# One wide matmul in place of two narrow ones in the MLP and convolution projections of a decoder trunk

## The chip, the cores and the metric

The kernel runs on one core of one Trainium2 chip. The metric is device time in microseconds (us) of one execution; the medians below are over several executions. TensorE (PE in the tables) does the matmuls and has its weight loads listed apart (PEld); VectorE is DVE, ScalarE is ACT, GpSimd is POOL, and SP is the engine that issues most transfers. Matmul results go to PSUM, the accumulation memory, here in tiles of 512 fp32 columns (one bank) or 1024 (two banks); everything else lies in SBUF.

## The reference, cut to what matters

Four layers on 256 tokens of 1024 features. Each layer has a token mixer (stick-breaking attention, short convolution, gated linear attention, attention again) and an MLP with 4096 hidden features, each with an RMS norm before and after.

```python
def short_conv_mixer(xn, w_in, conv_w, w_out):
    bcu = xn @ w_in                                  # 1024 -> 3 x 1024
    b_gate, c_gate, u = jnp.split(bcu, 3, axis=-1)
    h = c_gate * u
    ...
    conv = sum(conv_w[i] * hp[:, i:i + s] for i in range(CONV_WIDTH))
    return (b_gate * conv) @ w_out

def squared_relu_mlp(xn, w_up, w_down):              # 1024 -> 4096 -> 1024
    return jnp.square(jax.nn.relu(xn @ w_up)) @ w_down
```

Everything is fp32. All weights, 213 MB, are read from HBM once.

## The kernel before, in words

**Precision.** TensorE is fed with a rounded fp32 format (fp32r). To keep fp32 accuracy each operand is split in two: hi is the value rounded to fp32r, lo is the rest. A product x·w is then three matmuls, hi(w)·hi(x), hi(w)·lo(x) and lo(w)·hi(x), added up in PSUM. Weights arrive as raw tiles of 128x1024 by transfers on SP (L197); `emit_upto` (L193) casts each on ScalarE to hi (L202) and subtracts on VectorE to get lo (L203), in two halves of 512 columns. The splits run six tiles ahead (LA), in rings of nine hi and nine lo tiles.

**Two ways to project.** `x_stat` (L307) keeps a 128x128 piece of x (or of the hidden features) stationary and streams 512 columns of weights; the results go to an acc tile of 1024 columns (two banks). `w_stat` (L358, steps from L346) keeps 128x128 pieces of the weights stationary and streams the 256 tokens of x; one unit makes 256 features for all 256 tokens in a wk tile (one bank): the two halves of 128 features lie side by side, and for each of 8 feature blocks k and each half j there are three matmuls of 256 columns, 48 in all. x lies transposed in two tiles, xth (its hi) and xtl (its lo).

**PSUM.** There are three acc tiles and two wk tiles, eight banks in all, and nothing else lies in PSUM. Tiles are handed out to whoever comes next once their last reader is done. The transposes (L262) that turn x or the hidden features also go through wk tiles, four of 128 columns to a tile.

**MLP (`ffn`, L395 on).** The hidden features come in eight groups of 512. Groups 0 and 1 are made by `up_x` with x stationary, then squared, and transposed. Groups 2 to 7 are made by `up_w`, two `w_stat` units each (k = 0, 1). After each unit ScalarE takes Relu out of the wk tile (L430), VectorE squares it (L431), ScalarE squares it again into hi (L434), VectorE subtracts for lo (L435). `down(g)` multiplies a group's hidden features by its part of the second weight and adds up in two acc tiles, one for each half of the tokens, from the first group to the last. `up_w(g)` is followed by `down(g - 2)`, so a group's features are wanted two groups later. In the last layer the second token half's sum takes one half of an acc tile and one half of the third.

**Convolution (`conv`, L594 on).** b is projected with x stationary and transposed (`turn`, L605). Then come four groups of 256 features: unit c in a wk tile, copied out by ScalarE (L618), and unit u in the other, multiplied by c on VectorE straight out of PSUM (L625). The three taps follow (L630, L632), the product with b (L636) and the split (L638), and after the fourth group the output projection. The attention and gated layers also use `w_stat` (for q and k).

**Order.** The code is written out in program order; a scheduler in the framework then orders each engine's instructions by priority and by its estimate of when operands and tiles are ready. Each engine runs its own row strictly in order. PE, DVE and ACT therefore meet at the tiles: PE waits for a wk or acc tile until it is copied out, and a copy waits for the unit's last matmul.

Of the kernel before, what the change touches and what calls it, by code (L numbers as in the profile page):

```python
# [9 lines left out]
F32 = mybir.dt.float32  # L10
F32R = mybir.dt.float32r
I32 = mybir.dt.int32
AF = mybir.ActivationFunctionType
ALU = mybir.AluOpType
PSUM = bass.MemoryType.PSUM

P = 128
D = 1024
UNIT = 1024
KT = D // P  # L20
SEQ = 256
# [40 lines left out]
def hybrid_kernel(ctx: ExitStack, tc: tile.TileContext, x, norm_gains, sb_w_qkv, sb_w_o,  # L62
# [5 lines left out]
    nc = tc.nc  # L68
# [6 lines left out]
    def pool(name, bufs, **kw):  # L75
        return ctx.enter_context(tc.tile_pool(name=name, bufs=bufs, **kw))

    cp = pool("const", 1)
# [10 lines left out]
    def nm(s):  # L89
        cnt[0] += 1  # L90
        return f"{s}{cnt[0]}"

    def T(pl, shape, dt, tag):
        return pl.tile(shape, dt, tag=tag, name=nm(tag))
# [4 lines left out]
    def acc_tile():  # L99
        return T(accp, [P, 1024], F32, "acc")  # L100

    def wk_tile():
        return T(wkp, [P, 512], F32, "wk")

    def slot(shape=(P, 1024), dt=F32):
        return T(slots, list(shape), dt, "s")

    def scratch():
        return slot()

    def mm(o, l, r, start, stop):
        nc.tensor.matmul(out=o, lhsT=l, rhs=r, start=start, stop=stop, skip_group_check=True)  # L112
# [39 lines left out]
    for kind, l in phases:  # L152
# [14 lines left out]
        elif kind == "sb":  # L167
            w = sb_w_qkv[l // 3]
# [5 lines left out]
        elif kind == "conv":  # L174
            w = conv_w_in[0]
# [5 lines left out]
        else:  # L181
            w = gla_w_in[0]
# [24 lines left out]
    def need(key, j=0):  # L207
        emit_upto(index[(key, j)] + 1 + LA)
        return ready[(key, j)]
# [11 lines left out]
    def split(hi, lo, src):  # L221
        nc.scalar.copy(out=hi, in_=src)  # L222
        nc.vector.tensor_tensor(out=lo, in0=src, in1=hi.bitcast(F32), op=ALU.subtract)
# [30 lines left out]
            if dst is not None:  # L254
                (nc.sync, nc.scalar)[n].dma_start(out=dst[:, cs], in_=h[t][:, cs])

    xth = T(cp, [P, KT, SEQ], F32R, "xth")
    xtl = T(cp, [P, KT, SEQ], F32R, "xtl")

    def transposes(src, dst, n):  # L260
        for j in range(n):
# [42 lines left out]
    def banks(acc):  # L304
        return [acc[:, 0:512], acc[:, 512:1024]]
# [52 lines left out]
    def w_stat(o, key):  # L358
        for _ in w_stat_steps(o, key):
            pass  # L360

    class Fill:


# [12 lines left out]
    def u_pair():  # L377
        return slot((P, 4, SEQ), F32R), slot((P, 4, SEQ), F32R)
# [16 lines left out]
    def ffn(l, finish, final=False):  # L395
        us = {}
        accs = [None, None]
        parts = {}

        def up_x():  # L400
            prs = [u_pair() for _ in range(XG)]
            for g in range(XG):
                us[g] = prs[g]
            for t in range(NT):
                acc = acc_tile()
                lh, ll = xs(t)
                for k in range(4):
                    un = [need((l, "up", g, k)) for g in range(XG)]
                    ws = [[(hi[:, a, :], lo[:, a, :]) for hi, lo in un] for a in range(2)]
                    for j, _ in enumerate(x_stat_steps(banks(acc), lh[2 * k:], ll[2 * k:], ws, k == 0, k == 3)):  # L410
                        if 2 * k + j + 1 == TURN[1]:
                            turn_pending()
                r = scratch()
                nc.scalar.activation(out=r, in_=acc, func=AF.Relu)
                s = scratch()
                nc.vector.tensor_tensor(out=s, in0=r, in1=r, op=ALU.mult)
                for g in range(XG):
                    w = wk_tile()
                    transposes(s[:, g * 512:], w, 4)
                    sl = (slice(None), slice(0, 4), slice(t * P, (t + 1) * P))  # L420
                    split(us[g][0][sl], us[g][1][sl], w.rearrange("p (a b) -> p a b", b=P))

        def up_w(g):
            us[g] = u_pair()
            for k in range(2):
                w = wk_tile()
                w_stat(w, (l, "up", g, k))
                rs = scratch()
                r, s = rs[:, 0:512], rs[:, 512:1024]
                nc.scalar.activation(out=r, in_=w, func=AF.Relu)  # L430
                nc.vector.tensor_tensor(out=s, in0=r, in1=r, op=ALU.mult)  # L431
                hi = us[g][0][:, 2 * k:2 * k + 2, :].rearrange("p a b -> p (a b)")
                lo = us[g][1][:, 2 * k:2 * k + 2, :].rearrange("p a b -> p (a b)")
                nc.scalar.activation(out=hi, in_=r, func=AF.Square)  # L434
                nc.vector.tensor_tensor(out=lo, in0=s, in1=hi.bitcast(F32), op=ALU.subtract)  # L435

        def down(g, ts_):
            for k in range(4):
                if 4 * (g - 6) + k == TURN[0]:
                    turn_pending()  # L440
                for t in ts_:
                    if accs[t] is None:
                        accs[t] = acc_tile()
                        parts[t] = banks(accs[t])
                        if final and t == NT - 1:
                            parts[t][1] = acc_tile()[:, 0:512]
                    sl = slice(t * P, (t + 1) * P)
                    x_stat(parts[t], [us[g][0][:, k, sl]], [us[g][1][:, k, sl]], [wide((l, "dn", g), k)],
                           g == 0 and k == 0, g == 7 and k == 3)

        up_x()
        for g in range(XG, 8):
            up_w(g)
            if g >= 2:
                down(g - 2, (0, 1))
        for t in range(NT):
            if final and t == NT - 1:
                for n in range(2):
                    for g in (6, 7):
                        for k in range(4):  # L460
                            sl = slice(t * P, (t + 1) * P)
                            x_stat(parts[t][n:], [us[g][0][:, k, sl]], [us[g][1][:, k, sl]],
                                   [wide((l, "dn", g), k)[n:n + 1]], False, g == 7 and k == 3)
            else:
                down(6, (t,))
                down(7, (t,))
            finish(parts[t] if final and t == NT - 1 else [accs[t]], t)
# [126 lines left out]
    def conv(l, finish):  # L594
        cw = T(cp, [P, 3, KT], F32, "cw")
        nc.gpsimd.dma_start(out=cw, in_=conv_w[0].rearrange("i (k p) -> p i k", p=P))
        bt = [slot((P, 4, SEQ)) for _ in range(2)]
        bs = []
        for t in range(NT):
            acc = x_proj(t, (l, "b"))  # L600
            b = scratch()
            nc.scalar.copy(out=b, in_=acc)
            bs.append(b)

        def turn(t):  # L605
            for half in range(2):
                w = wk_tile()
                transposes(bs[t][:, half * 512:], w, 4)
                nc.vector.tensor_copy(out=bt[half][:, :, t * P:(t + 1) * P], in_=w.rearrange("p (a b) -> p a b", b=P))  # L609

        turn(0)
        us = [u_pair(), u_pair()]
        for g in range(4):
            w = wk_tile()
            w_stat(w, (l, "c", g))
            cs = scratch()
            c, y = cs[:, 0:512], cs[:, 512:1024]
            nc.scalar.copy(out=c, in_=w)  # L618
            if g == 0:
                turn(1)  # L620
            w = wk_tile()
            w_stat(w, (l, "u", g))
            hp = slot((P, 2, SEQ + 2))
            nc.gpsimd.memset(hp[:, :, 0:2], 0.0)
            nc.vector.tensor_tensor(out=hp[:, :, 2:SEQ + 2], in0=w.rearrange("p (a b) -> p a b", b=SEQ),  # L625
                                    in1=c.rearrange("p (a b) -> p a b", b=SEQ), op=ALU.mult)
            for j in range(2):
                f = 2 * g + j
                yj = y[:, j * SEQ:(j + 1) * SEQ]
                nc.scalar.activation(out=yj, in_=hp[:, j, 0:SEQ], func=AF.Copy, scale=cw[:, 0, f:f + 1])  # L630
                for i in (1, 2):
                    nc.vector.scalar_tensor_tensor(out=yj, in0=hp[:, j, i:i + SEQ], scalar=cw[:, i, f:f + 1],  # L632
                                                   in1=yj, op0=ALU.mult, op1=ALU.add)
            btv = bt[g // 2][:, 2 * (g % 2):2 * (g % 2) + 2, :].rearrange("p a b -> p (a b)")
            yb = scratch()[:, 0:512]
            nc.vector.tensor_tensor(out=yb, in0=y, in1=btv, op=ALU.mult)  # L636
            sl = (slice(None), slice(2 * (g % 2), 2 * (g % 2) + 2), slice(None))
            split(us[g // 2][0][sl].rearrange("p a b -> p (a b)"), us[g // 2][1][sl].rearrange("p a b -> p (a b)"), yb)  # L638
        out_proj(l, us, finish)
# [207 lines left out]
    k, l = phases[0]  # L847
# [64 lines left out]
```

## Time and profile before

| | |
|---|---|
| median of three runs | 1217.8 us (1217.74 to 1217.99) |
| profiled execution | 1217.98 us |
| its span, first to last instruction | 1216.1 us |
| PE busy | 1190.9 us, 98% of the span, 7260 matmuls |
| weight loads (PEld) busy | 1051.6 us, 86% |
| VectorE, ScalarE, GpSimd busy | 63%, 55%, 4% |
| mean granted TensorE clock | 0.998 of 2.4 GHz |
| HBM read | 213.01 MB, 176 GB/s over the span |

The profile is of one execution. A matmul's row gives its start and how long it lasted to the last result; successive matmuls overlap, so a stream's speed is read from the distance between starts, or from the length of an unbroken run of matmuls divided by their number. The chain that ended last is followed back from the last instruction, at each step to what released it. A row names output and inputs without buffer numbers, `wk<-xth,hi` being a matmul into a wk tile that streams xth against a stationary hi.

### The profile page before, as it was taken

Reading aid. Unit: us, or ns where it says so; the run is one execution under the profiler, and the core shown is the slowest. Engines: PE = TensorE matmul, PEld = TensorE weight load, DVE = VectorE, ACT = ScalarE, POOL = GpSimd, SP = SyncE. Lnnn points to the kernel's source line nnn. Section 1 sums busy time; section 2 is a strip of 40 time slices with the busy share of each in tenths; the row PEclk is TensorE's granted clock in tenths of the full one; section 3 lists DMA queues with packets and bytes.
Section 4 is the critical chain, followed back from the end, with each engine's and each line's share of the span. In section 5 each row is a group of like instructions: output and inputs, shape, how many; then the busy total and the mean of one; then the engine's idle time right before and its main releaser. Section 6 shows DMA issues by size and latency. Waiting matters only on the chain.

```text
span 1216.1 us, 18811 instructions
## 1 busy us (share of the span) xinstructions
PE 1190.9 (98%) x7260; PEld 1051.6 (86%) x7260; DVE 770.4 (63%) x1203; ACT 670.2 (55%) x1192; POOL 52.4 (4%) x90
## 2 busy tenths in 40 slices
PE   5999999999999999999999999999999999999997
PEld 4998889988889888998789888989988988899986
DVE  6675776555677766555656677655558666765552
ACT  5687565554555465554464645645545876564451
POOL 2000100000100100000200110000000000000000
PEclk9999999999999999999999999999999999999999
DMA  7843457566466556666564346665647452666640
GB/s 237 273 123 120 139 191 217 185 190 222 140 208 191 173 187 215 189 191 208 162 221 133 94 135 223 192 196 185 208 140 236 128 157 95 198 211 194 188 153 35
DMA packets 123083, 215.28 MB, mean 177 GB/s; under 512 B 7729, under 2 KB 85681, under 8 KB 122994
## 3 DMA queue, kind: packets, MB, share of 16 engines
q1 hardware_dynamic: 122434, 213.28, 55.8%
q8 instruction: 57, 0.93, 0.3%
q0 software_dynamic: 128, 0.21, 0.1%
q10 hardware_dynamic: 432, 0.59, 0.1%
q14 instruction: 32, 0.26, 0.1%
HBM read 213.01 MB, written 1.05 MB: 176 GB/s over the span
## 4 chain that ended last, share of the span: by engine, by line
PE 93%; issue 3%; ACT 1%; DVE 1%; DMA 1%; POOL 1%; SPq 0%; DVEq 0%; POOLq 0%; ACTq 0%
PE acc L112 54%; PE wk L112 37%; PE wk L262 2%; DMA raw<-in_sb_w_qkv_dram 1%; DMA raw<-in_gla_w_in_dram 0%; ACT hi L202 0%; POOL sm L232 0%; ACT s L559 0%; ACT s L237 0%; POOL s L784 0%; DVE lo L203 0%; DVE s L279 0%; POOL sm L229 0%; DVE h L253 0%; ACT s L797 0%
## 5 line engine op out<-in xcount | busy, mean ns | idle before, releaser
L203 DVE TENSOR_TENSOR lo<-raw,hi 128x512 fp32r<-128x512 f32 x768 | 500.9, 688 | 265.0 <-ACT hi L202 261.1
L202 ACT CAST hi<-raw 128x512 fp32r<-128x512 f32 x768 | 442.7, 618 | 355.2 <-PE wk L112 169.1
L112 PE MATMUL acc<-hi,s 128*128 128x512 f32 x1280 | 355.1, 392 | 0.0
L112 PE MATMUL wk<-xth,hi 128*128 128x256 f32 x1216 | 342.1, 281 | 0.4 <-DVE s L609 0.4
L112 PE MATMUL wk<-xtl,hi 128*128 128x256 f32 x1216 | 341.9, 281 | 0.0
L112 PE MATMUL wk<-xth,lo 128*128 128x256 f32 x1216 | 341.3, 281 | 0.0
L112 PEld LDWEIGHTS acc<-hi,s 128*128 128x128 f32 x1280 | 237.4, 188 | 48.9 <-ACT s L222 1.3
L112 PEld LDWEIGHTS wk<-xth,hi 128*128 128x128 f32 x1216 | 229.3, 189 | 2.5 <-issue 0.7
L112 PEld LDWEIGHTS wk<-xtl,hi 128*128 128x128 f32 x1216 | 229.1, 188 | 1.3 <-issue 0.2
L112 PEld LDWEIGHTS wk<-xth,lo 128*128 128x128 f32 x1216 | 229.5, 189 | 0.2 <-issue 0.2
L112 PE MATMUL acc<-lo,s 128*128 128x512 f32 x640 | 199.7, 390 | 0.0
L112 PEld LDWEIGHTS acc<-lo,s 128*128 128x128 f32 x640 | 120.0, 188 | 25.3
L112 PE MATMUL acc<-hi,xth 128*128 128x512 f32 x288 | 94.0, 404 | 1.2 <-ACT xth L222 1.2
L112 PE MATMUL acc<-hi,xtl 128*128 128x512 f32 x288 | 93.0, 401 | 0.0
L112 PE MATMUL acc<-lo,xth 128*128 128x512 f32 x288 | 92.3, 400 | 0.0
L112 PEld LDWEIGHTS acc<-hi,xtl 128*128 128x128 f32 x288 | 54.7, 190 | 12.9
L112 PEld LDWEIGHTS acc<-lo,xth 128*128 128x128 f32 x288 | 54.6, 191 | 12.9
L112 PEld LDWEIGHTS acc<-hi,xth 128*128 128x128 f32 x288 | 53.9, 191 | 13.4 <-ACT xth L222 1.6
L250 DVE TENSOR_TENSOR s<-acc,s 128x1024 f32<-128x1024 f32 (+1 forms) x17 | 19.7, 1161 | 65.3 <-ACT s L237 65.0
L229 POOL TENSOR_SCALAR sm<-sm 128x1 f32<-128x1 f32 (+1 forms) x32 | 15.2, 476 | 1053.8 <-ACT s L237 1049.1
L112 PE MATMUL acc<-s,s 128*128 128x256 f32 (+3 forms) x316 | 51.5, 336 | 2.3 <-ACT s L559 1.8
L237 ACT ACTIVATE s<-acc 128x1024 f32<-128x1024 f32 (+1 forms) x17 | 16.6, 974 | 63.3 <-PE acc L112 63.3
(102 smaller groups left out, 762.9 us busy)
## 6 DMA issues: line engine op xcount, KB each, us to landing
raw<-in_ffn_w_up_dram SPq DMA_DIRECT2D x128, 512.0 KB, 3.8
raw<-in_ffn_w_down_dram SPq DMA_DIRECT2D x128, 512.0 KB, 3.6
raw<-in_sb_w_qkv_dram SPq DMA_DIRECT2D x48, 512.0 KB, 4.9
raw<-in_conv_w_in_dram SPq DMA_DIRECT2D x24, 512.0 KB, 4.4
raw<-in_gla_w_in_dram SPq DMA_DIRECT2D x24, 512.0 KB, 4.4
s<-in_norm_gains_dram SPq DMA_DIRECT2D x16, 512.0 KB, 5.1
raw<-in_sb_w_o_dram SPq DMA_DIRECT2D x16, 512.0 KB, 3.7
raw<-in_conv_w_out_dram SPq DMA_DIRECT2D x8, 512.0 KB, 3.6
```

Of the source, the lines that this page charges most:

```text
L112: nc.tensor.matmul(out=o, lhsT=l, rhs=r, start=start, stop=stop, skip_group_check=True)
L202: nc.scalar.copy(out=hi[:, cs], in_=raw[:, cs])
L203: nc.vector.tensor_tensor(out=lo[:, cs], in0=raw[:, cs], in1=hi[:, cs].bitcast(F32), op=ALU.subtract)
L229: nc.gpsimd.tensor_scalar(out=v, in0=ss, scalar1=EPS, scalar2=None, op0=ALU.add)
L237: nc.scalar.activation(out=scratch()[:, 0:src.shape[1]], in_=src, func=AF.Square, scale=1.0 / 32.0, accum_out=ss)
L250: nc.vector.tensor_tensor(out=ag[:, cs], in0=a, in1=g[:, cs], op=ALU.mult)
L262: nc.tensor.transpose(out=dst[:, j * P:(j + 1) * P], in_=src[:, j * P:(j + 1) * P], identity=ident)
```

## The change

x's hi and lo now lie side by side in one tile xt, 512 columns for each feature block, and xth and xtl are views of it. A new helper `w_wide` makes the same unit as `w_stat` with two matmuls in place of three for each k and j: hi(w) against both parts of x in one matmul of 512 columns, then lo(w) against hi(x), 256 columns, added onto the second half. The unit now takes two banks, one for each half j of its features, and its result is the sum of the first and the second half of a bank. `w_sum` makes that sum: ScalarE copies the second half out of PSUM and VectorE adds the first half to it. The unit's PSUM is an acc tile (k = 0 of each MLP group; c and u of the convolution) or both wk tiles (k = 1). The MLP's units then take max(y, 0)·y in one VectorE operation and split it with a cast and a subtraction. In the last layer the k = 1 units stay as they were and one wk tile holds the half sum that lay in the third acc tile. q and k of the attention and gated layers are not changed.

```diff
-    xth = T(cp, [P, KT, SEQ], F32R, "xth")
-    xtl = T(cp, [P, KT, SEQ], F32R, "xtl")
+    xt = T(cp, [P, KT, 2, SEQ], F32R, "xt")
+    xth, xtl = xt[:, :, 0, :], xt[:, :, 1, :]
...
+    def w_wide(key, two):
+        if two:
+            parts = [wk_tile().rearrange("p (j b) -> p j b", j=1) for _ in range(2)]
+            o = [p[:, 0, :] for p in parts]
+        else:
+            parts = [acc_tile().rearrange("p (j b) -> p j b", j=2)]
+            o = [parts[0][:, j, :] for j in range(2)]
+        for k in range(KT):
+            hi, lo = need(key, k // 4)
+            for j in range(2):
+                cs = slice(j * P, (j + 1) * P)
+                mm(o[j], hi[:, k % 4, cs], xt[:, k, :, :].rearrange("p c s -> p (c s)"), k == 0, False)
+                mm(o[j][:, SEQ:2 * SEQ], lo[:, k % 4, cs], xth[:, k, :], False, k == KT - 1)
+        return parts
+
+    def w_sum(parts, out, small_out):
+        n = 2 // len(parts)
+        for j, part in enumerate(parts):
+            js = slice(j * n, (j + 1) * n)
+            nc.scalar.copy(out=small_out[:, js, :], in_=part[:, :, SEQ:2 * SEQ])
+            nc.vector.tensor_tensor(out=out[:, js, :], in0=part[:, :, 0:SEQ], in1=small_out[:, js, :], op=ALU.add)
...
             for k in range(2):
-                w = wk_tile()
-                w_stat(w, (l, "up", g, k))
...
+                if final and k == 1:
...
+                    continue
+                parts = w_wide((l, "up", g, k), k == 1)
+                ys = scratch().rearrange("p (c j b) -> p c j b", c=2, j=2)
+                y, s = ys[:, 0, :, :], ys[:, 1, :, :]
+                w_sum(parts, y, s)
+                nc.vector.scalar_tensor_tensor(out=s, in0=y, scalar=0.0, in1=y, op0=ALU.max, op1=ALU.mult)
+                split(us[g][0][:, 2 * k:2 * k + 2, :], us[g][1][:, 2 * k:2 * k + 2, :], s)
...
-                            parts[t][1] = acc_tile()[:, 0:512]
+                            parts[t][1] = wk_tile()
...
-            w = wk_tile()
-            w_stat(w, (l, "c", g))
...
-            nc.scalar.copy(out=c, in_=w)
+            halves = lambda ap: ap.rearrange("p (a b) -> p a b", b=SEQ)
+            w_sum(w_wide((l, "c", g), False), halves(c), halves(y))
             if g == 0:
                 turn(1)
-            w = wk_tile()
-            w_stat(w, (l, "u", g))
+            ub = scratch()
+            u = halves(ub[:, 0:512])
+            w_sum(w_wide((l, "u", g), False), u, halves(ub[:, 512:1024]))
...
-            nc.vector.tensor_tensor(out=hp[:, :, 2:SEQ + 2], in0=w.rearrange("p (a b) -> p a b", b=SEQ),
-                                    in1=c.rearrange("p (a b) -> p a b", b=SEQ), op=ALU.mult)
+            nc.vector.tensor_tensor(out=hp[:, :, 2:SEQ + 2], in0=u, in1=halves(c), op=ALU.mult)
```

Three places show what this does to the order. In these rows a number behind a name tells tiles apart and has no other meaning.

PE at the start of the first MLP, before: acc_1789 and acc_1804 are the two sums of down(0), the two L262 rows transpose group 0 and group 1 for the second half of the tokens, and wk_1649 is the first up unit.

```order
L112 MATMUL acc_1789<-hi_1530,s_1431 128x512 x2
L112 MATMUL acc_1789<-lo_1531,s_1431 128x512 x2
L112 MATMUL acc_1789<-hi_1530,s_1432 128x512 x2
L262 MATMUL wk_1633<-cf_84,s_1631 128x128 x4
L262 MATMUL wk_1640<-cf_84,s_1631 128x128 x4
L112 MATMUL acc_1789<-hi_1652,s_1431 128x512
L112 MATMUL acc_1804<-hi_1522,s_1431 128x512 x2
L112 MATMUL acc_1804<-lo_1523,s_1431 128x512 x2
L112 MATMUL acc_1789<-hi_1652,s_1431 128x512
L112 MATMUL acc_1789<-lo_1653,s_1431 128x512
L112 MATMUL wk_1649<-xth_93,hi_1466 128x256
```

PE at the same place now, in two pieces: around the transposes (acc_1648 is the first up unit, k = 0), and where the second unit, k = 1, begins in wk_1703 and wk_1704.

```order
L112 MATMUL acc_1648<-xt_93,lo_1466 128x256
L112 MATMUL acc_1648<-xt_93,hi_1465 128x512
L263 MATMUL wk_1632<-cf_84,s_1630 128x128 x4
L263 MATMUL wk_1639<-cf_84,s_1630 128x128 x4
L112 MATMUL acc_1648<-xt_93,lo_1466 128x256
L112 MATMUL acc_1648<-xt_93,hi_1473 128x512
```

```order
L112 MATMUL acc_1648<-xt_93,hi_1473 128x512
L112 MATMUL acc_1648<-xt_93,lo_1474 128x256
L112 MATMUL wk_1703<-xt_93,hi_1493 128x512
L112 MATMUL wk_1703<-xt_93,lo_1494 128x256
L112 MATMUL wk_1704<-xt_93,hi_1493 128x512
```

The matmuls of down(0) that stood around the transposes have moved behind the up units; fifteen matmuls of the first up unit stand ahead of the transposes and seventeen behind them, and the k = 1 unit takes over the two wk tiles that the transposes leave.

PE in the convolution at the second turn of b, before: wk_3401 is unit c of group 0, wk_3480 its unit u.

```order
L112 MATMUL wk_3401<-xth_93,lo_3251 128x256
L262 MATMUL wk_3468<-cf_84,s_3383 128x128 x4
L262 MATMUL wk_3474<-cf_84,s_3383 128x128 x4
L112 MATMUL wk_3480<-xth_93,hi_3264 128x256
L112 MATMUL wk_3480<-xtl_94,hi_3264 128x256
```

The same place now, with the units c and u in acc_3239 and acc_3303.

```order
L112 MATMUL acc_3239<-xt_93,hi_3087 128x512
L112 MATMUL acc_3239<-xt_93,lo_3088 128x256
L263 MATMUL wk_3290<-cf_84,s_3220 128x128 x4
L263 MATMUL wk_3296<-cf_84,s_3220 128x128 x4
L112 MATMUL acc_3303<-xt_93,hi_3101 128x512
L112 MATMUL acc_3303<-xt_93,lo_3102 128x256
```

The order is the same; the units no longer share the two wk tiles with the transposes.

VectorE behind the first two up units, before: L431 squares, L435 subtracts, L203 are weight splits.

```order
L431 TENSOR_TENSOR s_1714<-s_1714 128x512
L203 TENSOR_TENSOR lo_1793<-raw_1790,hi_1792 128x512
L435 TENSOR_TENSOR s_1648<-s_1714,s_1647 128x512
L203 TENSOR_TENSOR lo_1814<-raw_1811,hi_1813 128x512 x2
L203 TENSOR_TENSOR lo_1834<-raw_1831,hi_1833 128x512
L431 TENSOR_TENSOR s_1784<-s_1784 128x512
L203 TENSOR_TENSOR lo_1834<-raw_1831,hi_1833 128x512
L435 TENSOR_TENSOR s_1648<-s_1784,s_1647 128x512
```

VectorE there now: L386 adds the halves, L469 squares, L223 subtracts.

```order
L386 TENSOR_TENSOR s_1697<-acc_1648,s_1697 128x512
L203 TENSOR_TENSOR lo_1765<-raw_1762,hi_1764 128x512
L469 SCALAR_TENSOR_TENSOR s_1697<-s_1697 128x512
L203 TENSOR_TENSOR lo_1786<-raw_1783,hi_1785 128x512
L223 TENSOR_TENSOR s_1647<-s_1697,s_1646 128x512
L203 TENSOR_TENSOR lo_1786<-raw_1783,hi_1785 128x512
L386 TENSOR_TENSOR s_1753<-wk_1703,s_1753 128x256
L203 TENSOR_TENSOR lo_1806<-raw_1803,hi_1805 128x512
L386 TENSOR_TENSOR s_1753<-wk_1704,s_1753 128x256
L203 TENSOR_TENSOR lo_1806<-raw_1803,hi_1805 128x512
L469 SCALAR_TENSOR_TENSOR s_1753<-s_1753 128x512
```

One addition per unit is new, in two pieces for a k = 1 unit, each with a copy on ScalarE ahead of it, and the weight splits stand between the steps as before.

## Rows read from the trace of the kernel before

**Rows 1.** The page's busy times: us (share of the span), instructions.

```profile
PE 1190.9 (98%) x7260; PEld 1051.6 (86%) x7260; DVE 770.4 (63%) x1203; ACT 670.2 (55%) x1192; POOL 52.4 (4%) x90
```

**Rows 2.** The page's chain that ended last: shares by engine, then by line.

```profile
PE 93%; issue 3%; ACT 1%; DVE 1%; DMA 1%; POOL 1%; SPq 0%; DVEq 0%; POOLq 0%; ACTq 0%
PE acc L112 54%; PE wk L112 37%; PE wk L262 2%; DMA raw<-in_sb_w_qkv_dram 1%; DMA raw<-in_gla_w_in_dram 0%; ACT hi L202 0%; POOL sm L232 0%; ACT s L559 0%; ACT s L237 0%; POOL s L784 0%; DVE lo L203 0%; DVE s L279 0%; POOL sm L229 0%; DVE h L253 0%; ACT s L797 0%
```

**Rows 3.** The page's groups: first of three narrow kinds; busy, mean ns | idle before.

```profile
L112 PE MATMUL wk<-xth,hi 128*128 128x256 f32 x1216 | 342.1, 281 | 0.4 <-DVE s L609 0.4
```

**Rows 4.** The chain by time: start us, length us, what ran.

```profile
186.33 11.39 PE wk L112 x96
197.73 10.91 PE acc L112 x48
...
331.28 11.23 PE acc L112 x48
```

**Rows 5.** Timeline of PE, attention of layer 0: start, length in us, instruction.

```profile
119.67 0.53 PE L112 MATMUL acc<-s,cr 128*128 128x256 f32 x2
120.03 0.28 PE L112 MATMUL acc<-s,onesr 128*128 128x256 f32 x1
120.15 0.52 PE L112 MATMUL acc<-s,cr 128*128 128x256 f32 x2
120.51 0.28 PE L112 MATMUL acc<-s,onesr 128*128 128x256 f32 x1
```

**Rows 6.** Timeline of PE, an earlier head pair of the same layer.

```profile
103.72 0.39 PE L112 MATMUL acc<-s,cr 128*128 128x512 f32 x1
103.95 0.28 PE L112 MATMUL wk<-xth,hi 128*128 128x256 f32 x1
104.06 0.28 PE L112 MATMUL acc<-s,onesr 128*128 128x256 f32 x1
...
105.23 0.51 PE L112 MATMUL acc<-s,cr 128*128 128x256 f32 x2
105.58 0.28 PE L112 MATMUL acc<-s,onesr 128*128 128x256 f32 x1
```

**Rows 7.** Timeline of PE at the start of the first MLP's up units.

```profile
165.38 1.06 PE L262 MATMUL wk<-cf,s 128*128 128x128 f32 x8
166.20 1.21 PE L112 MATMUL acc<-hi,s 128*128 128x512 f32 x3
167.24 0.63 PE L112 MATMUL acc<-lo,s 128*128 128x512 f32 x2
```

**Rows 8.** Timeline of VectorE at the same place.

```profile
166.95 1.28 DVE L223 TENSOR_TENSOR s<-wk,s 128x512 fp32r<-128x512 f32 x2
```

**Rows 9.** Timeline of PE, start of the convolution; in brackets, idle before and its releaser.

```profile
345.18 0.38 PE L112 MATMUL wk<-xth,hi 128*128 128x256 f32 x1 [0.41 <-DVE s L609]
...
352.16 0.66 PE L262 MATMUL wk<-cf,s 128*128 128x128 f32 x4 [0.64 <-ACT s L618]
```

**Rows 10.** Stretches: length; PE, PEld, DVE, ACT, POOL busy; clock, DMA share, GB/s.

```profile
352.80:392.70 39.90, 39.90 (x338) 39.90 (x337) 28.72 (x50) 20.64 (x39) 0.00 (x0) 1.00 0.58 176
...
197.70:220.00 22.30, 22.30 (x146) 20.41 (x145) 12.77 (x20) 11.17 (x21) 0.00 (x0) 1.00 0.62 189
```

**Rows 11.** Groups by form, whole span: operations that price the evictions; busy, mean ns.

```profile
L625 DVE TENSOR_TENSOR s<-wk,s 128x512 f32<-128x512 f32 x4 | 2.8, 692 | 3.9 <-PE wk L112 3.9
L277 DVE SCALAR_TENSOR_TENSOR s<-h,sm,s 128x512 f32<-128x512 f32 x2 | 1.4, 750 | 0.7 <-DMA s<-in_norm_gains_dram 0.7
...
L618 ACT COPY s<-wk 128x512 f32<-128x512 f32 x4 | 2.3, 581 | 0.0
```

**Rows 12.** The convolution's end: VectorE's last subtraction, and the chain's output projection.

```profile
397.62 0.69 DVE L223 TENSOR_TENSOR s<-s,s 128x512 fp32r<-128x512 f32 x1 [0.69 <-ACT s L222]
...
392.69 19.07 PE acc L112 x84
```

More of the change, by code (lines that the diff above doesn't have):

```diff
@@ L425, in up_w @@
             for k in range(2):
-                w = wk_tile()
-                w_stat(w, (l, "up", g, k))
[L428 to L435, printed above, removed]
+                if final and k == 1:
+                    w = wk_tile()
+                    w_stat(w, (l, "up", g, k))
+                    rs = scratch()
+                    r, s = rs[:, 0:512], rs[:, 512:1024]
+                    nc.scalar.activation(out=r, in_=w, func=AF.Relu)
+                    nc.vector.tensor_tensor(out=s, in0=r, in1=r, op=ALU.mult)
+                    hi = us[g][0][:, 2 * k:2 * k + 2, :].rearrange("p a b -> p (a b)")
+                    lo = us[g][1][:, 2 * k:2 * k + 2, :].rearrange("p a b -> p (a b)")
+                    nc.scalar.activation(out=hi, in_=r, func=AF.Square)
+                    nc.vector.tensor_tensor(out=lo, in0=s, in1=hi.bitcast(F32), op=ALU.subtract)
+                    continue
[5 more added lines that the diff above has]
+                split(us[g][0][:, 2 * k:2 * k + 2, :], us[g][1][:, 2 * k:2 * k + 2, :], s)
         def down(g, ts_):
```

## The prediction, made before the changed kernel ran

> **What bounds the kernel now.** I read the page's busy times first: PE is busy for 98% of the span, VectorE for 63%, ScalarE for 55% [rows 1]. A busy PE may still stand on pipelined matmuls, so next comes the chain that ended last: 93% of it is PE, 54% matmuls into acc tiles and 37% into wk tiles, all issued at L112 [rows 2]. From about 20 us to 1200 us, PE therefore runs one matmul behind the other and sets the time. What counts is then not how long one matmul lasts (its 0.28 or 0.39 us overlap the next) but the distance between starts, which the chain by time gives: 96 narrow matmuls (256 columns) of two up units in 11.39 us, **118.7 ns each**; 48 of 512 columns in a down step in 10.91 us, **227.3 ns**; 48 of 512 columns that have x as the stationary side in 11.23 us, **234.0 ns** [rows 4]. At the full clock, 2.4 GHz (the mean granted clock is 0.998), 256 columns take 106.7 ns and 512 take 213.3, so there is a fixed part per matmul of 12.0, 14.0 and 20.7 ns. That fixed part is all that the change can save: the columns stay.
>
> **The change, part by part.**
> *Matmuls.* Each of the three kinds of narrow matmul (hi by xth, hi by xtl, lo by xth) stands 1216 times in the trace [rows 3]. The new helper serves 42 up units (six groups, two units, four layers, less the six k = 1 units of the last layer) and 8 convolution units, with 16 triples in each: 50 x 16 = 800 triples become pairs of one 512 column and one 256 column matmul. 800 matmuls and 800 weight loads go. A triple now costs 3 x 118.7 = 356.0 ns.
>
> A pair of 512 and 256 columns in regular alternation does not stand in the trace. Bounds: the settled streams give 227.3 + 118.7 = 346.0 ns [rows 4]; with the dearer of the two 512 prices, 352.7. Nearest in kind are the attention's suffix sums, where single 512s stand among 256s: 256 then 512 takes 0.36 us twice (119.67 to 120.03, 120.15 to 120.51) [rows 5], and 512 then 256 takes 0.34 us (103.72 to 104.06), 256 then 512 0.35 us (105.23 to 105.58) [rows 6]: 352.5 ns on average. In alternation the pattern is regular, as in the settled streams, but lengths change at each step, as in the mixed rows. I take **350 ns**, between 346 and 352.5 and a little nearer to the mixed ones. The saving is 6.0 ns x 800 = **4.8 us**, between 8.0 us at 346 and a loss of 0.8 to 3.2 us at 357 to 360, which the mixed rows do not exclude.
>
> On this fixed part the Trainium skill (TensorE: Matmul & The Clock Gate, section Back-to-back issue gap) says otherwise: N/2.4 plus about 2.5 ns. By that an estimate for the triple is 327.5 ns and for the pair 325.0, a gain of 2.0 us in all. The trace differs, with a fixed part of 12 to 21 ns [rows 4], so the page's price is not used.
>
> *Waits at the start of an MLP.* Today the two transposes of step t = 1 (165.38) are followed by matmuls of down that need what is copied out of these transposes: the next five starts, from 166.20, should be 227 ns apart, but the first three take until 167.24, 1.04 us for 0.68 [rows 7]. In the new order the first up unit, now in an acc tile, stands on both sides of the transposes and needs nothing of them: 0.36 us x 4 layers = **1.4 us** less. What is late next: the k = 1 unit takes both wk tiles, which the transposes hold until VectorE's second subtraction ends at 166.95 + 1.28 = 168.23 [rows 8], 1.8 us after the transposes end (166.44). Before it come 17 matmuls of the first unit, 8 x 350 + 119 = 2.9 us. That covers it with 1.1 us to spare.
>
> *Waits at the start of the convolution.* PE waits 0.41 us for the copy out of a wk tile before unit c0, and 0.64 us for ScalarE's copy out of c0's wk tile before the second pair of transposes [rows 9]. With c0 in an acc tile, neither buffer is wanted there: **1.05 us** less. The weights of c0 were split before those copies, so nothing else is known to be late. If some other wait comes, these two terms (2.45 us in all) are what it can take back.
>
> *Evictions.* An up unit had on ScalarE a Relu and a Square, on VectorE a product and a subtraction; it gets a copy and a cast on ScalarE, and on VectorE an addition more. The prices: 0.58 us for a copy of 128x512 out of PSUM, 0.69 for a two-input VectorE operation out of PSUM, up to 0.75 for the three-operand form [rows 11]. So VectorE gets about 0.75 us per up unit, 1.5 us per group (a little more for k = 1, which is copied and added in two pieces); it is busy for 12.77 of 22.30 us there [rows 10] and comes to 14.5. In the convolution each group of c and u gets 1.4 us on VectorE, at 28.72 of 39.90 us now for 3.5 groups [rows 10], so about 33.5 of 39 us. Both are hidden under PE. The results of an up unit are wanted two groups later, behind 11 us of down. The tightest place is the end of the convolution: the last subtraction ends at 397.62 + 0.69 = 398.31, and PE wants it after 36 of the 84 matmuls that start at 392.69, 8.2 us on, at 400.9 [rows 12]. The new copy and addition, with a weight split between, add about 1.5 us to 2.6 us of slack. I cost all evictions at nothing; without that cover this place would cost what exceeds the slack, under 1 us.
>
> *Layout, queues.* xt holds hi and lo of x side by side; its writers and readers keep their shapes. The order of the weight transfers on SP stays the same, and these run at 0.62 of the DMA engines in the up stretch [rows 10]: nothing.
>
> *Sum* against the profiled execution, 1217.98 us (span 1216.1): 1217.98 - 4.8 - 1.4 - 1.05 = 1210.73. The median of the runs, 1217.8, is 0.18 us below that execution, so the forecast is **1210.6 us**; the rivals are reckoned from the median too.
>
> **The rivals.**
> *A: the alternation settles as well as the long streams,* 346 ns for a pair, as the down steps do after their first few matmuls. For it: a regular pattern. Against it: no mixed stretch shows it steadily. 8.0 + 2.45 us less: 1207.3.
> *B: the 512 column matmul costs what it costs with x on the stationary side,* 234.0, a pair 352.7 ns [rows 4]. For it: the mean of the mixed rows is the same; against it: here x moves and the weights stand, as in the settled narrow stream. 2.6 + 2.45 us less: 1212.7.
> *B2: only 2 to 3 ns go with the matmul, the rest of the fixed part with the columns;* the pair then costs about 353.5 ns, 2.0 + 2.45 us less: 1213.4. Against it: 14.0 ns at 512 columns and 12.0 at 256 in the settled streams [rows 4]. The section of the Trainium skill named above would give this time.
> *C: the change does not do what it says:* the fixed part goes with the columns alone. 512 columns then cost 2 x 118.7 = 237.4 ns, not far from the 234.0 of the third stream [rows 4], and a pair 356 to 358; only the waits go. For it also: 0.36 us for such pairs [rows 5]. At 357 ns 0.8 us more, less 2.45: 1216.1 (1215.4 to 1217.0), within 0.2% of before but for its lower edge.
> *D, slower: alternation is dearer than the triple.* The place is every pair, the price what exceeds 356.0 ns. Rows 5 show 0.36 us for a pair, which by the rounding of the start times may be anything from 350 to 370. At 364: 800 x 8 = 6.4 us more, less 2.45: 1221.7. It decides over 0.2% from (2.4 + 2.45)/0.8 = 6.1 ns on, at 362 ns for a pair. Against it: rows 6, at 0.34 and 0.35.
>
> **How the numbers follow.** A measurement of this kernel can tell about 0.2% (2.4 us) from no change. Forecast 0.40, A 0.22, B 0.14, B2 0.06, C 0.12, D 0.06. Faster by more than 0.2% are the forecast, A, B and B2: 0.82. Within it C: 0.12. Slower D: 0.06. The range takes in A with a pair of 344 ns (9.6 us, if the 512 keeps the 12.0 ns of the narrow stream), which gives 1205.7, B and B2, and reaches halfway into C: **1205.5 to 1216.5**.
>
> **What would show it.** In the changed trace the up unit (32 matmuls) should take about 5.6 us in place of 5.7, so that a group's two units last 11.2 us where they lasted 11.39; this alone decides between the forecast (11.20), A (11.07), B and B2 (11.29, 11.31), C (11.4) and D (11.65). The count of PE's matmuls should fall by about 800. At an MLP's start the three matmuls behind the transposes should no longer stretch, and the k = 1 unit should begin without a wait; if PE waits there for VectorE, the cover of 2.9 us was too short. At the convolution both waits should be gone, and the output projection should run through its 36th matmul without a gap. VectorE's share in the up stretch should rise to about 0.65 of the time, with PE still without gaps. The prediction would be wrong if PE showed new waits on wk or acc tiles in every group, or if a pair came out beyond 357 ns.

## The result and the profile after

The changed kernel takes **1205.7 us** (median of 4 runs, 1205.0 to 1207.1) beside 1217.8 for the kernel before: ratio 0.990, 95% interval 0.989 to 0.991. That is 12 us faster; the forecast was 7.2 us faster, and the median lies only 0.2 us inside the lower edge of its range, 1205.5. The profiled execution took 1205.45 us (span 1203.6) at a granted clock of 0.997.

The page's busy times and the shares of its chain, to be read beside [rows 1] and [rows 2]:

```profile
PE 1180.6 (98%) x6460; PEld 1010.5 (84%) x6460; DVE 803.0 (67%) x1271; ACT 673.9 (56%) x1214; POOL 51.8 (4%) x90
...
PE 93%; DMA 2%; issue 1%; ACT 1%; DVE 1%; POOL 1%; SPq 0%; DVEq 0%; POOLq 0%; ACTq 0%
```

PE has 800 matmuls and 800 weight loads fewer, as the change says, and is as full as before: 98% of a shorter span, 93% of the chain. VectorE rose from 63 to 67%; no new wait of PE for it appeared (the list of waits below).

The chain by time, the view of [rows 4]: start, length, what ran. The first lines are the first MLP with its first groups; then come the convolution and a unit of the last layer that kept the narrow form.

```profile
164.57 2.90 PE acc L112 x17
167.47 5.55 PE wk L112 x32
173.02 16.44 PE acc L112 x80
189.46 5.55 PE wk L112 x32
195.01 16.44 PE acc L112 x80
...
340.66 5.55 PE acc L112 x32
...
347.09 57.92 PE acc L112 x308
...
1048.61 5.63 PE wk L112 x48
```

A unit of 16 pairs takes 5.55 us, **346.9 ns a pair**, in an acc tile (340.66) as in wk tiles. An MLP step of 80 is a down (10.89) and a unit (5.55). A group lasts 21.99 us, where it took 11.39 + 10.91 = 22.30 [rows 4]. The 308 matmuls from 347.09 on are the seven remaining units of the convolution (7 x 5.55 = 38.85) and 84 of its output projection: one piece, without a gap.

PE at the start of the first MLP, the place of [rows 7]:

```profile
163.51 1.06 PE L263 MATMUL wk<-cf,s 128*128 128x128 f32 x8
164.33 0.36 PE L112 MATMUL acc<-xt,lo 128*128 128x256 f32 x1
164.53 0.40 PE L112 MATMUL acc<-xt,hi 128*128 128x512 f32 x1
164.76 0.28 PE L112 MATMUL acc<-xt,lo 128*128 128x256 f32 x1
...
167.31 0.39 PE L112 MATMUL wk<-xt,hi 128*128 128x512 f32 x1
```

and VectorE there, the place of [rows 8]:

```profile
165.48 1.29 DVE L223 TENSOR_TENSOR s<-wk,s 128x512 fp32r<-128x512 f32 x2 [0.31 <-ACT s L222]
```

Pairs stand on both sides of the transposes, and the matmuls behind these no longer stretch. The wk tiles are free at 165.48 + 1.29 = 166.77; the k = 1 unit takes them at 167.31, without a wait.

The waits of PE that the profile lists, over the whole span (us in total, times, longest):

```profile
PE wk L263 <- DVE s L278: 8.1, 1, 8.1
PE wk L263 <- DVE s L280: 3.3, 2, 2.7
PE acc L112 <- ACT s L594: 1.8, 2, 0.9
PE wk L263 <- DVE s L838: 1.4, 2, 1.2
PE acc L112 <- ACT xt L222: 0.9, 1, 0.9
PE acc L112 <- POOL s L712: 0.5, 1, 0.5
```

The two waits of [rows 9] are gone and no new line took their place. The first line is the start of the program, ahead of the first transposes; before it was 9.6 us.

### The profile page after: what moved, and what is told of

Its sections match the earlier page's. It is cut to its first block, busy times and chain, and to the rows that moved or that the text cites. A ratio compares the mean times of both kernels' runs of the same rounds, so it can differ in the third digit from the quotient of the medians.

```text
span 1203.6 us, 17278 instructions
## 1 busy us (share of the span) xinstructions
PE 1180.6 (98%) x6460; PEld 1010.5 (84%) x6460; DVE 803.0 (67%) x1271; ACT 673.9 (56%) x1214; POOL 51.8 (4%) x90
## 3 DMA queue, kind: packets, MB, share of 16 engines
HBM read 213.01 MB, written 1.05 MB: 178 GB/s over the span
## 4 chain that ended last, share of the span: by engine, by line
PE 93%; DMA 2%; issue 1%; ACT 1%; DVE 1%; POOL 1%; SPq 0%; DVEq 0%; POOLq 0%; ACTq 0%
PE acc L112 68%; PE wk L112 23%; PE wk L263 2%; DMA raw<-in_gla_w_in_dram 1%; DMA h<-in_x_dram 1%; ACT s L237 0%; ACT hi L202 0%; POOL sm L232 0%; ACT s L594 0%; DVE s L280 0%; POOL s L818 0%; DVE lo L203 0%; POOL sm L229 0%; DVE h L253 0%; ACT s L831 0%
## 5 line engine op out<-in xcount | busy, mean ns | idle before, releaser
L203 DVE TENSOR_TENSOR lo<-raw,hi 128x512 fp32r<-128x512 f32 x768 | 504.9, 688 | 219.2 <-ACT hi L202 215.7
L112 PE MATMUL wk<-xt,hi 128*128 128x256 f32 (+1 forms) x1120 | 252.7, 310 | 0.0
L112 PE MATMUL wk<-xt,lo 128*128 128x256 f32 x704 | 197.0, 280 | 0.0
L112 PEld LDWEIGHTS wk<-xt,hi 128*128 128x128 f32 x1120 | 182.8, 188 | 13.4 <-issue 0.9
L112 PE MATMUL acc<-xt,hi 128*128 128x512 f32 x512 | 179.3, 392 | 0.0
L112 PE MATMUL acc<-hi,xt 128*128 128x512 f32 x576 | 167.1, 403 | 0.9 <-ACT xt L222 0.9
L112 PE MATMUL acc<-xt,lo 128*128 128x256 f32 x512 | 143.5, 280 | 0.0
L112 PEld LDWEIGHTS wk<-xt,lo 128*128 128x128 f32 x704 | 132.4, 188 | 0.2 <-issue 0.2
L112 PEld LDWEIGHTS acc<-hi,xt 128*128 128x128 f32 x576 | 108.1, 190 | 26.2 <-ACT xt L222 1.3
L112 PEld LDWEIGHTS acc<-xt,hi 128*128 128x128 f32 x512 | 96.1, 188 | 21.1
L112 PEld LDWEIGHTS acc<-xt,lo 128*128 128x128 f32 x512 | 96.3, 188 | 0.9
```

What stands on the lines that cost most here:

```text
L203: nc.vector.tensor_tensor(out=lo[:, cs], in0=raw[:, cs], in1=hi[:, cs].bitcast(F32), op=ALU.subtract)
```

## Experiments

All are built on the changed kernel, except the one on the layout. Every ratio is to the kernel before, run beside the experiment. "Changed" below is its two measurements, 1205.7 and 1206.5 us.

**1. The matmuls narrow again, all else as changed.** New tiles, order and evictions stay; each pair becomes a triple of 256 columns.

```diff
-mm(o[j], hi[:, k % 4, cs], xt[:, k, :, :].rearrange("p c s -> p (c s)"), k == 0, False)
+mm(o[j][:, 0:SEQ], hi[:, k % 4, cs], xth[:, k, :], k == 0, False)
+mm(o[j][:, SEQ:2 * SEQ], hi[:, k % 4, cs], xtl[:, k, :], False, False)
```

> The changed kernel, but with three matmuls of 256 columns in place of the 512 and the 256: hi by the hi of x onto the first half, hi by the lo of x and lo by the hi of x onto the second. PSUM tiles, evictions and order stay as changed. Theory: the gain is a fixed part that each matmul costs, so the pair of 347 ns becomes a triple of 352 to 356 again, 800 x 5 to 9 ns = 4 to 7 us more: about 1210 to 1213 us, and the waits at the start of the MLPs and of the convolution stay away. Rival: the gain came from the tiles and the new evictions; then the time stays within 1 us of 1205.7.

Measured: 1214.3 us, ratio 0.9973 (0.9964 to 0.9983). Its chain by time in the first MLP:

```profile
190.98 5.70 PE wk L112 x48
196.68 16.61 PE acc L112 x96
```

Units of 5.70 us, a group of 22.31: inside the groups everything that the change brought is gone, with its evictions still there. So the wide matmul is the whole of the groups' gain, some 8 us (1214.3 less 1206), a little more than the theory's 4 to 7; the remaining 3.6 us to the kernel before (1217.9 beside it) lie outside these groups.

**2. The up units alone; the convolution as before.** (`w_wide` and `w_sum` are taken out of the convolution, whose lines are again those of the kernel before.)

> The changed kernel with the convolution's units as before (three narrow matmuls in wk tiles, u multiplied straight out of PSUM). Theory: the convolution gave 128 pairs x 9 ns = 1.2 us and the two waits at its start, 1.05 us in the profile's waits, so 1205.7 + 2.2 = about 1208 us, and both waits are back. Rival: its longer eviction chain took something back, or the waits were worth nothing; then 1206 to 1207 us.

Measured: 1209.1 us, ratio 0.9931 (0.9908 to 0.9954): by the medians the convolution's part is about 3 us, but the four runs lie up to 3.2 us apart. Both waits are back, in PE's waits:

```profile
PE wk L263 <- ACT s L653: 0.6, 1, 0.6
PE wk L112 <- DVE s L644: 0.4, 1, 0.4
```

The traces say it more sharply. From the first transposes of the convolution to the first ones behind its output projection, PE takes 67.86 us here (340.92 to 408.78), as in the kernel before (343.73 to 411.59), and 65.22 in changed (339.63 to 404.85). Eight units with 16 pairs make 1.2 us of the 2.64; the other 1.5 are what the waits cost, more than the 1.05 us at which their rows stand.

**3. The layout alone**, in the kernel before.

```diff
-xth = T(cp, [P, KT, SEQ], F32R, "xth")
-xtl = T(cp, [P, KT, SEQ], F32R, "xtl")
+xt = T(cp, [P, KT, 2, SEQ], F32R, "xt")
+xth, xtl = xt[:, :, 0, :], xt[:, :, 1, :]
```

> The kernel before with the hi and lo of x side by side in one tile, and nothing else. In the changed kernel's profile the first transposes start 1.4 us earlier (8.12 us in place of 9.56) and the rest of the start follows. Theory: that is no effect of the layout but differs between builds or runs, in the landing of the first transfers; time 1217.8 us within 0.5 us on average. Rival: the one tile in place of two lets the start run earlier; about 1216 us, with the first transposes at 8.1 us.

Measured: 1217.8 us, ratio 1.000 (0.999 to 1.001). The layout by itself is worth nothing that these runs could show (about 1 us). The rival's sign did not show either: the first transposes waited 8.9 us, not 8.1.

**4. x, the split weights and the hidden features all moved to a multiple of 64 bytes.** The tiles lie behind each other in a partition. Counted by the sizes of those ahead of them, the changed kernel has x 32 bytes off a multiple of 64, the split weights (`hi`, `lo`) and the slots of hidden features on one. A larger small tile ahead of x, and a larger one between x and the rest, move them.

```diff
-mhalf = T(cp, [P, 8], F32, "mhalf")
+mhalf = T(cp, [P, 16], F32, "mhalf")
-cw = T(cp, [P, 3, KT], F32, "cw")
+cw = T(cp, [P, 4, KT], F32, "cw")[:, 0:3, :]
```

> The changed kernel with two small constant tiles made wider, so that the tile of x and all weight and slot tiles begin at a multiple of 64 bytes in each partition; so far x begins 32 bytes off and the others on one. Theory: the 512 column matmuls with x stationary start 233 to 234 ns apart and those of down 227 because the stationary side is off the multiple; then the 864 of them come to 227 ns, 864 x 6.5 = 5.6 us less: about 1200 us. Rival: the distance has another cause (the kind of stream, what ran before); time 1205.7 us, distances as they were.

Measured: 1210.9 us, ratio 0.9943 (0.9925 to 0.9961): **slower** than changed by 4 to 5 us. The theory fell. In the chain by time, 54 matmuls of layer 0's projections, then a unit and a step of the MLP, and a narrow unit of the last layer:

```profile
136.06 12.49 PE acc L112 x54
...
191.97 5.62 PE wk L112 x32
197.58 16.48 PE acc L112 x80
...
1053.44 5.76 PE wk L112 x48
```

Projections with x as the stationary side hardly moved: 12.49 us for 12.55 in changed (at 133.66), 1 ns each. What moved was the pair, 351 ns for 346.9: a place that was thought good made the new stream dearer. Pairs make 800 x 4.3 ns = 3.4 us of it, and the six narrow units of the last layer 0.8 (5.76 for 5.63 us); the rest was not divided further.

**5. The changed kernel again**, beside the next ones.

> The changed kernel once more, unaltered. In its first profile the start (up to the first transposes) took 8.12 us, in five other profiles of kernels with the same start 8.9 to 9.6 us. Theory: the start varies from run to run with the landing of the first transfers, and the first four runs had luck; then the median here is about 1206.5 us (1206 to 1208), and a profile with the first transposes near 9.3 us has a span about 1.2 us longer, all of it at the start. Rival: the start of this kernel is always early; 1205.7 us again and 8.1 us.

Measured: 1206.5 us, ratio 0.9910 (0.9895 to 0.9925). Its profiled execution was the longest of its four, 1208.67 us. The chain of that one at the same unit, and PE's first wait:

```profile
170.33 5.55 PE wk L112 x32
...
PE wk L263 <- DVE s L278: 9.8, 1, 9.8
```

The same program is here 2.9 us later at its first k = 1 unit than in the execution above (167.47), 1.7 of it from the wait ahead of the first transposes, 9.8 for 8.1. So the start varies, as the theory says, but by more than its 1.2 us. VectorE's timeline shows where it comes from. PE's first transposes wait for this step of the norm, here in the execution above:

```profile
7.31 1.41 DVE L278 SCALAR_TENSOR_TENSOR s<-h,sm,s 128x512 f32<-128x512 f32 x2 [0.83 <-DMA s<-in_norm_gains_dram]
```

In this execution it begins at 8.96, again right behind the landing of the norm's gains, and the first weights land later too: their cast on ScalarE begins at 11.15 for 9.32. In the profile of the kernel before these two stand at 8.75 and 11.07, near the late ones. The difference of the two profiles' spans of before and after (12.5 us) therefore holds some luck of the start.

**6. Every new copy and addition made twice.**

```diff
-nc.scalar.copy(out=small_out[:, js, :], in_=part[:, :, SEQ:2 * SEQ])
-nc.vector.tensor_tensor(out=out[:, js, :], in0=part[:, :, 0:SEQ], in1=small_out[:, js, :], op=ALU.add)
+for _ in range(2):
+    nc.scalar.copy(out=small_out[:, js, :], in_=part[:, :, SEQ:2 * SEQ])
+    nc.vector.tensor_tensor(out=out[:, js, :], in0=part[:, :, 0:SEQ], in1=small_out[:, js, :], op=ALU.add)
```

> The changed kernel with ScalarE's copy and VectorE's addition of each wide unit made twice, with the same result: per up unit about 0.58 us more on ScalarE and 0.69 on VectorE, in 42 up units and 8 convolution units. Theory: the evictions are hidden under PE everywhere but perhaps at the end of the convolution, where the slack is 1 us; the time stays within 1.5 us of the changed kernel. Rival: the evictions are on the path at least where tiles are handed on; 50 x 1.3 = 65 us of added work would then show as 5 us or more.

Measured: 1207.6 us, ratio 0.9913 (0.9898 to 0.9928), not to be told from changed. VectorE in the stretch of a group rose from 14.1 to 15.4 us of 22 (length; PE, PEld, DVE busy and on as in [rows 10]):

```profile
197.13:219.12 21.99, 21.99 (x114) 18.78 (x113) 15.38 (x27) 12.55 (x26) 0.00 (x0) 1.00 0.65 192
```

The group lasts 21.99 us all the same, and so does the convolution's piece of 308 matmuls (57.92 us in changed):

```profile
349.29 57.94 PE acc L112 x308
```

The evictions are hidden, with room for as many again.

**7. x off a multiple of 64 in another way,** with a tile of 96 bytes ahead of it.

```diff
-mhalf = T(cp, [P, 8], F32, "mhalf")
+mhalf = T(cp, [P, 24], F32, "mhalf")
```

> The run with all tiles at a multiple of 64 bytes took 1210.9 us, with pairs at 350.8 ns in place of 347.5 and narrow matmuls at 119.2 in place of 118.1. Here x is moved on by 32 bytes more, so that it begins 32 bytes off a multiple of 64 again, at another place, while weights and slots stay on the multiple. Theory: what counts for the streamed x is whether it lies on the multiple; pairs return to 347 to 348 ns and the time to 1206 to 1207 us. Rival: the difference has another cause (other places of weights and slots, the run); pairs stay at 350 to 351 ns, 1210 to 1211 us.

Measured: 1206.3 us, ratio 0.9906 (0.9891 to 0.9921), units of 5.55 us again. So what counts is not the shift of addresses as such, but where it ends within 64 bytes; experiments 9 to 11 ask whether that is x's own place.

**8. The wide form in the attention too,** for the units of q (an acc tile) and of k (both wk tiles).

```diff
-w = wk_tile()
-yield from w_stat_steps(w, (l, "q", g))
+parts = []
+yield from w_wide_steps(parts, (l, "q", g), False)
...
+    w_sum(parts, wv, ys[:, 1, :, :])
```

> The changed kernel with the same wide form for the q and k units of the two attention layers too: q in the third acc tile, k in both wk tiles, 16 units with 16 pairs each. Theory: a fixed part per matmul is saved wherever PE is the bound, so 256 pairs x 9 ns = 2.3 us less than the changed kernel, 1204 us, if the added copy and addition on the attention's chain of ScalarE and VectorE stay hidden. Rival: the k unit takes both wk tiles right behind the q unit, and the attention's chain on ScalarE and VectorE, which PE waits for there today (1.8 us at L594), grows; no gain or a loss of up to 5 us.

Measured: 1212.2 us, ratio 0.9956 (0.9939 to 0.9973): a loss of 6 us against changed, though 256 more matmuls are gone (6204 for 6460). PE's waits, those that are new or grew:

```profile
PE acc L112 <- ACT s L604: 4.5, 6, 1.4
PE acc L112 <- DVE s L223: 3.2, 6, 0.7
...
PE wk L112 <- DVE s L392: 0.7, 2, 0.4
```

In changed the first of these stood at 1.8 us (L594), the others not at all: 6.6 us more in all. In the attention ScalarE and VectorE are what PE is fed by: the extra copy and addition lie on the path there, and the shorter matmuls only make PE wait sooner. The rival's wk tiles are the last line, the smallest part.

**9 to 11. Which relative place is the dear one.** One theory had the price hang on x's own place, the other on whether both operands have the same place within 64 bytes. The edit of 9 is the first pair of lines of experiment 4 (`mhalf`) alone, that of 10 the second pair (`cw`) alone, and 11 has the second pair and a tile of 32 bytes between the weights and the slots:

```diff
+pad = T(padp, [P, 8], F32, "pad")
```

> The changed kernel with x on a multiple of 64 bytes and the weight and slot tiles 32 bytes off. Known so far for the wide pair (x streams, weights stand): x off and weights on 347 to 348 ns, both on 350.8 ns. Theory 1: only the streamed side counts, off being cheaper: pairs at 351 ns, and the streams whose weights move (down, x projections, 227 and 233 ns) get cheaper by a few ns, 1800 to 2600 matmuls x 2 to 4 ns = 4 to 10 us less from there. Theory 2: what counts is that the two sides differ: pairs at 347 ns, down as before (227 ns, both sides alike again). Rival to both: no pattern, each stream with a price of its own.

> The changed kernel with x, weights and slots all 32 bytes off a multiple of 64. Theory 1 (only the streamed side counts): pairs at 347 ns, down cheaper than 227 ns. Theory 2 (the two sides must differ): pairs at 351 ns, 1210 us, down as before at 227 ns, since its sides stay alike.

> The changed kernel with x and the weights 32 bytes off a multiple of 64 and the slots on it, so that down streams weights that are off against hidden features that are on. Theory 1 (only the streamed side counts): pairs at 347 ns, down cheaper than 227 ns, time below 1206 us. Theory 2 (the two sides must differ): pairs at 351 ns, down cheaper than 227 ns. Should down get dearer, neither holds for streams of 512 columns.

Measured: 1206.3 us (ratio 0.9903, 0.9886 to 0.9919), 1210.6 (0.9936, 0.9922 to 0.9951) and 1220.6 (1.0022, 1.0013 to 1.0032). The chain by time of 9, of 10 and of 11 (where L113 is the same line), a unit and the last down each:

```profile
190.24 5.55 PE wk L112 x32
...
1176.38 10.89 PE acc L112 x48
```

```profile
192.15 5.62 PE wk L112 x32
...
1181.16 10.89 PE acc L112 x48
```

```profile
193.96 5.62 PE wk L113 x32
...
1192.04 11.21 PE acc L113 x48
```

Put together ("on": on a multiple of 64 bytes; "off": 32 beside it):

| kernel | x | weights | hidden | pair, ns | down, ns | us |
|---|---|---|---|---|---|---|
| changed, and 7 | off | on | on | 347 | 227 | 1206 |
| 9 | on | off | off | 347 | 227 | 1206.3 |
| 4 | on | on | on | 351 | 227 | 1210.9 |
| 10 | off | off | off | 351 | 227 | 1210.6 |
| 11 | off | off | on | 351 | 233.5 | 1220.6 |

(A pair is a unit over 16, a down the last 48 matmuls over 48; for 4 these took 10.89 us.) For the pair, x's own place doesn't matter; it is cheap where x and the weights differ and dear where they are alike. For down the sign is the other way: cheap where weights and hidden features are alike, dear where they differ, which one kernel alone shows. There 1536 down matmuls (48 to a group, 32 groups) x 6.6 ns = 10.1 us are the whole difference between 10 and 11. The third stream, projections with x stationary, follows neither: 54 of them in layer 0 take 12.55 us in changed, 12.55 in 9, 12.49 in 4, 12.50 in 10 and 12.55 in 11. So the theory of relative place holds for the pair and not as a general rule; why the streams want different things stays open.

## Why the prediction was right, and where its size was off

*What bounds the kernel.* Right. PE ran matmul behind matmul before and does after, so what each costs from start to start, times the count, came out of the end time.

*The pairs.* The mechanism held: a fixed part goes with each matmul, and 800 of them went. **The size was off at one step: the 350 ns taken for a pair.** Measured is 346.9, the sum of the two settled streams (346.0), which was rival A. Two units lasted 11.10 us; the forecast put its own case at 11.20 and A's at 11.07. By the units' rows the saving is (11.39 - 11.10)/32 = 9.1 ns a pair, 7.3 us in all; experiment 1 gives some 8; the prediction had 4.8. The mixed attention rows [rows 5, 6], on which 350 leaned, were a poor neighbour: single pairs, read at start times rounded to 0.01 us. They also have other operands, and experiments 4, 10 and 11 show that placement alone moves a pair by 4 ns; that this is why those rows came out at 352.5 was not tried. The forecast did not reckon with placement, and that the changed kernel lies at the cheap place is luck: at the dear one (experiments 4 and 10) a pair costs 351 ns, close to the 350 taken. What the kernel before would cost there was not tried.

*The rivals.* Units of 5.55 us rule out B, B2 and D (5.64, 5.66 and 5.82), and C as well, by which a unit would have stayed at 5.70, as it does with the triples of experiment 1. B2's time is also the one that a formula of the Trainium skill gives (TensorE: Matmul & The Clock Gate, section Back-to-back issue gap), an estimate of 2.0 us for the pairs; the section gives that formula for an isolated matmul, not for a stream of weight loads and matmuls. This trace does not agree with it, with 7.3.

*The MLP's start.* Right. The next unit's 17 matmuls take 2.90 us, as reckoned, and cover VectorE with 0.54 us to spare (1.1 was forecast: VectorE ended 1.8 us after the transposes before, 2.2 us after them now, 166.77 for 164.57). Behind the transposes one start is 0.08 us late (164.33 to 164.53, 0.20 for 0.12) where three together were 0.36 late [rows 7]. That this was a wait for what is copied out of the transposes shows, in the kernel before, in a weight load there that waits for ScalarE's copy:

```profile
166.68 0.30 PEld L112 LDWEIGHTS acc<-hi,s 128*128 128x128 f32 x2 [0.32 <-ACT s L222]
```

The other three starts show the same distances. This is 0.28 to 0.36 us at each of four starts, 1.1 to 1.4 in all.

*The convolution's start.* Right in place, somewhat small. The kernel before, first a line of PE's timeline, then lines of its chain by time:

```profile
343.73 1.03 PE L262 MATMUL wk<-cf,s 128*128 128x128 f32 x8
...
345.18 5.90 PE wk L112 x48
351.08 0.45 PE wk L262 x4
...
352.16 0.66 PE wk L262 x4
352.81 39.88 PE wk L112 x336
```

and the same in the changed kernel:

```profile
339.63 1.03 PE L263 MATMUL wk<-cf,s 128*128 128x128 f32 x8
...
346.21 0.87 PE wk L263 x8
```

From the start of the first transposes to the first unit behind the second ones it was 352.81 - 343.73 = 9.08 us and is 347.09 - 339.63 = 7.46. Of these 1.62 us the pair form of unit c0 is 0.15, so 1.47 us went with the waits, for a forecast of 1.05. The forecast took the bracketed idle time [rows 9] for the whole price. Here the second wait also cut the transposes in two pieces, 0.45 + 0.66 = 1.11 us, where they now take 0.87 in one: 0.24 us beyond the idle time. Unit c0, behind the first wait, took 5.90 us where the other units take 5.70: 0.20 more.

*Evictions, layout, queues at nothing.* Right, for evictions and layout by experiments 6 and 3; the queues had no experiment, and PE's list of waits shows none for a transfer. VectorE is busy for 14.12 of 21.98 us in a group's stretch (14.5 was forecast) and 32.72 of 38.80 in the convolution (33.5 of 39):

```profile
195.01:216.99 21.98, 21.98 (x113) 18.77 (x113) 14.12 (x23) 11.20 (x23) 0.00 (x0) 1.00 0.64 192
347.10:385.90 38.80, 38.80 (x225) 34.16 (x225) 32.72 (x58) 22.67 (x44) 0.10 (x1) 1.00 0.60 183
```

At its tightest place, the convolution's end, VectorE is done at 392.74 + 0.69 = 393.43:

```profile
392.74 0.69 DVE L223 TENSOR_TENSOR s<-s,s 128x512 fp32r<-128x512 f32 x1 [0.69 <-ACT s L222]
```

PE wants it 36 matmuls after 385.94, at about 394.1. The forecast's slack was 1.1 us, this is 0.7.

*The sum.* 7.3 for pairs, 1.1 to 1.4 at four MLP starts, 1.5 at the convolution: 9.9 to 10.2 of the 11.3 to 12.0 us measured. Against the forecast the pairs brought 2.5 us more and the waits 0.1 to 0.5. Of the narrow matmuls that are left, the six units of the last layer went from 5.70 to 5.63 us (1048.61 in the chain above), 0.4 us together; why is open. That makes 10.3 to 10.6.

The traces tell the rest from the start. Layer 0's projections come ahead of all the changed matmuls; the chain by time has them so, before and after:

```profile
135.50 12.57 PE acc L112 x54
```

```profile
133.66 12.55 PE acc L112 x54
```

They begin 1.84 us earlier already, by the luck of experiment 5. Of the 12.5 us between the spans 10.7 are left. In experiment 5's execution the span is 9.2 us shorter though these projections begin 1.02 later (136.52), which makes 10.2. So the change itself is worth 10.2 to 10.7 us in these traces, and the terms above account for it. The medians' 11.3 to 12.0 lie somewhat higher; that their starts make up the difference is likely and not shown, for only one run of each four was profiled.

## What to carry to other kernels

Where an engine is full, price its instructions by the distance from start to start in long unbroken runs, not by their duration and not by odd pairs in a mixed place; for a new regular pattern the sum of the settled streams was the better estimate. Matmuls that share a stationary tile are worth merging where the added work of eviction lies on engines that nobody waits for, and not worth it where the same engines feed PE, as in the attention. When thousands of matmuls stream, it is worth trying operands 32 bytes further on: here such moves cost nothing or up to 14 us, beside 12 for the whole change, and the changed kernel lay at one of the cheap places by luck.

## What was not expected of the hardware

Placement within 64 bytes changes a matmul's price by a few ns in these runs, with opposite signs for two streams: 347 or 351 ns for a pair with weights stationary, 227 or 233.5 for a down matmul of 512 columns with the hidden features stationary. No form of it that was tried beat the changed kernel. The wait ahead of the first transposes was 8.1 us in one execution of the changed kernel and 9.8 in another, as the first transfers landed earlier or later.
